# Gates and branch projections with tokens on partitions, their gated sum turned by PE chunk by chunk

## The chip, the cores and the metric

One Trainium2 chip; the kernel runs on one of its cores. PE (TensorE) multiplies matrices, DVE (VectorE) and ACT (ScalarE) work on elements, POOL (GpSimd) does little here, SP (SyncE) issues the loads. Each engine executes its own instructions in order and waits for others by semaphores. The metric is the time of one execution in microseconds (us), the median of three runs.

## The reference, cut to what matters

One layer over x of 256 tokens by 2048 features. h is the normed and modulated x; z = h @ w_in; three branches (mLSTM, differential attention, stick-breaking attention) work on parts of z and give out_m, out_d and out_s of 256 x 1024 each. The change concerns this part:

```python
        merged = (jax.nn.sigmoid(gm) * (out_m @ w_branch[l, 0])
                  + jax.nn.sigmoid(gd) * (out_d @ w_branch[l, 1])
                  + jax.nn.sigmoid(gs) * (out_s @ w_branch[l, 2]))
        x = x + gt1 * (merged @ w_out[l])
```

gm, gd and gs are the last three pieces of z, each 256 x 2048 (columns of w_in). A gated MLP with a depthwise convolution over tokens follows (w_up, w_down), and all of it is float32.

## The kernel before

**Matmuls.** A float32 product is made of three passes: each operand is split in hi, its value rounded to the matmul type fp32r, and lo, the rest; hi*hi, hi*lo and lo*hi are summed in PSUM. Activations are split once; `hh` and `hl` are the hi and lo of h, with features on partitions (16 row tiles of 128 features, 256 tokens each). Weights are streamed: `weights` loads 4 row tiles (4 x 128 rows, 512 columns, tile `raw`, 3 buffers) on SP's queue; ACT casts two row tiles at a time to `hi` (L324) and DVE subtracts to get `lo` (L326); hi and lo have 4 buffers each.

**gemm** makes 512 output columns in two banks of PSUM (pool `gp`, 3 banks) and has two forms. In "F" the output has features on partitions: 128 columns of the weights are the stationary operand and the 256 tokens of the activation stream past (L359). In "T" the output has tokens on partitions: 128 tokens of the activation are stationary and 512 columns of the weights stream past (L357). For one row tile of weights F has 4 column tiles x 3 products, T has 2 token tiles x 3 products. Apart from the last group of a gemm, the two row tiles of a hi/lo pair are done for all output tiles before the next pair.

**Order of the work.** The program emits gemms one after another; between them `tick` emits pieces of two queues: `side` (the generators `stick`, `diff` and `mlstm`, the attention work of the branches) and `ada` (steps that stream w_ada through DVE, L212, for the modulation vectors), at the rates in `rates`. A scheduler then puts every engine's instructions in order.

**Stages around the change**, after the first part of w_in: gates of gs (4 chunks of 512 columns, 16 row tiles each) beside stick and then diff; branch 2 (4 chunks, 8 row tiles each, activation `osh`, `osl`); the sigmoid of mo and the values mv of mLSTM (form T, two chunks each, the end of diff beside them); mq and mk with their convolution (form F); branch 1, each chunk with its gates of gd, beside mlstm; branch 0, each chunk with its gates of gm and, in `ada`, the row gt1; the output projection w_out (form T, 16 row tiles, activation `mgh`, `mgl`). The sum of the gated branches is kept in `mg`, which in `branch` with order 2 is split into mgh and mgl.

**Slots.** Ten large tiles, tags s0 to s9, are used again and again; a new tile in a slot waits until all readers of the old one are done. mg0 and mg1 lie in s8 and s9 (s9 is ez of stick before). od, the output of diff, lies in s2; the transposes `ptf` in `to_features` turn it into odh and odl; `mv` takes s2 next.

Of the kernel before, what the change touches and what calls it, by code (L numbers as in the profile page):

```python
# [12 lines left out]
AF = mybir.ActivationFunctionType  # L13
ALU = mybir.AluOpType
# [3 lines left out]
P = 128  # L18
S = 256
NT = S // P  # L20
D = 2048
KD = D // P
MW = 1024
KM = MW // P
# [11 lines left out]
C_GM, C_GD, C_GS = 10248, 12296, 14344  # L36
# [3 lines left out]
def kernel(  # L40
# [8 lines left out]
    w_ada, w_in, w_out, w_up, w_down = w_ada[0], w_in[0], w_out[0], w_up[0], w_down[0]  # L49
    w_branch = w_branch[0]  # L50
# [16 lines left out]
    def bank(name):  # L67
        return mx.tile([P, 512], F32, tag="mx", name=name)

    def wide(name):  # L70
        return tmp.tile([P, 512], F32, tag="wide", name=name, bufs=3)
# [7 lines left out]
    V, A, T = nc.vector, nc.scalar, nc.tensor  # L79


    ident = const.tile([P, P], F32, name="ident")
# [100 lines left out]
    def pump(queue, n):  # L183
        done = 0
        while queue and done < n:
            try:
                next(queue[0])
                done += 1
            except StopIteration:
                queue.popleft()  # L190

    def drain(queue):
        pump(queue, 1 << 30)
# [3 lines left out]
    def tick():  # L197
        for key, queue in (("ada", ada), ("side", side)):
            state[key] += rates[key]
            n = int(state[key])  # L200
            state[key] -= n
            pump(queue, n)
# [33 lines left out]
    def ada_first(k0):  # L236

        accs = [adap.tile([P, 512], F32, tag="acc", name="acc", bufs=2)]
        for q in range(4):
            raw = rawp.tile([P, 4, 512], F32, tag="raw", name="raw")  # L240
            step = 2 if k0 == 0 and q == 3 else 4
            for j in range(0, 4, step):
                for i in range(2):
                    r0, c0 = q * 512 + j * P, i * D + k0 * P
                    with tc.issue_after(state["load"].ins) if k0 else nullcontext():
                        load = nc.sync.dma_start(raw[:, j:j + step, i * 256:(i + 1) * 256],
                                                 w_ada[r0:r0 + step * P, c0:c0 + 256].rearrange("(k p) f -> p k f", p=P))
            if k0 == 0:
                state["load"] = load
            with tc.issue_after(state["first"].ins) if k0 == 2 and q == 0 else nullcontext():  # L250
                ada_mac(accs, raw, 4 * q, 4)
            yield
        ada_sums(accs, k0, 2)
# [58 lines left out]
    def weights(rows, nk, n, hold=None):  # L312
        if nk == 2:
            raw = adap.tile([P, 2, 512], F32, tag="ada", name="raw2")
        else:
            raw = rawp.tile([P, 4, 512], F32, tag="raw", name="raw")
        with tc.issue_after(state["load"].ins) if not state["started"] else nullcontext():
            state["started"] = True
            state["load"] = nc.sync.dma_start(raw[:, :nk, :n], rows.rearrange("(k p) f -> p k f", p=P))
        his, los = [], []  # L320
        for k0 in range(0, nk, 2):
            hi = hip.tile([P, 2, 512], F32R, tag="hi", name="hi")
            lo = lop.tile([P, 2, 512], F32R, tag="lo", name="lo")
            A.copy(hi[:, :, :n], raw[:, k0:k0 + 2, :n])  # L324
            with tc.issue_after(hold.ins) if hold else nullcontext():
                state["split"] = V.tensor_tensor(lo[:, :, :n], raw[:, k0:k0 + 2, :n], hi[:, :, :n].bitcast(F32),  # L326
                                                 ALU.subtract)
            his.append(hi)
            los.append(lo)
        return his, los  # L330

    def gemm(orient, act, W, row0, col0, n, kt0, kt1, hold=None, hold_all=False, acc=None):

        started = set() if acc is None or kt0 == 0 else {0, 1}
        if acc is None:
            acc = [gp.tile([P, 512], F32, tag="gp", name="gp") for _ in range(2)]
        ah, al = act
        nt = 2 if orient == "T" else n // P  # L340
        per = 1 if orient == "T" else 2

        def mms(t, ks, s0, wh, wl):
            if orient == "T":
                o, sl = acc[t][:, :n], slice(t * P, (t + 1) * P)
            else:
                o, sl = acc[t // 2][:, (t % 2) * S:(t % 2 + 1) * S], slice(t * P, (t + 1) * P)
            for w, acts in ((wh, (ah, al)), (wl, (ah,))):
                for k in ks:
                    wk = w[k // 2][:, k % 2, :]  # L350
                    for a in acts:
                        b = t // per
                        start = b not in started
                        started.add(b)
                        kw = dict(start=start, stop=s0 + k == kt1 - 1 and w is wl, skip_group_check=True)
                        if orient == "T":
                            T.matmul(o, lhsT=a(s0 + k)[:, sl], rhs=wk[:, :n], **kw)  # L357
                        else:
                            T.matmul(o, lhsT=wk[:, sl], rhs=a(s0 + k), **kw)  # L359

        for s0 in range(kt0, kt1, 4):
            nk = min(4, kt1 - s0)
            r0 = row0 + s0 * P
            wh, wl = weights(W[r0:r0 + nk * P, col0:col0 + n], nk, n, hold if s0 > kt0 or hold_all else None)
            last = s0 + nk >= kt1
            for ks in ([range(nk)] if last else [range(k0, k0 + 2) for k0 in range(0, nk, 2)]):
                for t in range(nt):
                    mms(t, ks, s0, wh, wl)
            if not last:
                tick()  # L370
        return acc

    def split(hi, lo, src):

        A.copy(hi, src)
        return V.tensor_tensor(lo, src, hi.bitcast(F32), ALU.subtract)
# [4 lines left out]
    hact = (lambda kt: hh[:, kt, :], lambda kt: hl[:, kt, :])  # L381
# [45 lines left out]
    h0 = ada_first(0)  # L427
# [351 lines left out]

    mg = []  # L780

    def mg_of(ch, b):
        return mg[ch // 2][:, (ch % 2) * 1024 + b * 512:(ch % 2) * 1024 + (b + 1) * 512]

    def gates(col_g, ch, dst):
        acc = gemm("F", hact, w_in, 0, col_g + ch * 512, 512, 0, KD)
        for b in range(2):
            A.activation(dst(ch, b), acc[b], AF.Sigmoid)
        tick()

    def branch(bi, col_g, act, order):
        for ch in range(4):
            if order == 0:
                sg = [mg_of(ch, 0), mg_of(ch, 1)]
            else:
                sg = [wide("sg"), wide("sg")]
                gates(col_g, ch, lambda c_, b: sg[b])
            accb = gemm("F", act, w_branch[bi], 0, ch * 512, 512, 0, KM)
            for b in range(2):
                d = mg_of(ch, b)  # L800
                V.tensor_tensor(sg[b], accb[b], sg[b], ALU.mult)
                if order:
                    V.tensor_tensor(d, d, sg[b], ALU.add)
                if order == 2:
                    h0 = (ch % 2) * 4 + 2 * b
                    split(mgh[ch // 2][:, h0:h0 + 2, :], mgl[ch // 2][:, h0:h0 + 2, :],
                          d.rearrange("p (a t) -> p a t", a=2))
            tick()


# [14 lines left out]
    rates["ada"] = 0.9  # L825
    mg.append(slot(8, "mg0"))
    for ch in range(2):
        gates(C_GS, ch, mg_of)
    drain(side)
    mg.append(slot(9, "mg1"))  # L830
    side.append(diff())
    rates["side"] = 2.6
    for ch in range(2, 4):
        gates(C_GS, ch, mg_of)
    branch(2, C_GS, stick.out, 0)
    drain(side)

# [3 lines left out]
    for ch in range(2):  # L841
        acc = gemm("T", hact, w_in, 0, C_MO + ch * 512, 512, 0, KD)
# [5 lines left out]
    for ch in range(2):  # L848
        acc = gemm("T", hact, w_in, 0, C_MV + ch * 512, 512, 0, KD)
# [5 lines left out]
    for t, col0, f0 in ((mqT, C_MQ, 0), (mkT, C_MK, 8)):  # L855
        for ch in range(2):
            acc = gemm("F", hact, w_in, 0, col0 + ch * 512, 512, 0, KD)
# [9 lines left out]
            for b in range(2):  # L867
                sg = wide("sg")
# [16 lines left out]
    ada.append(ada_row(2, gt1))  # L885
    rates["ada"] = 1.4
    branch(0, C_GM, mlstm.out, 2)


# [8 lines left out]
    for ch in range(4):  # L898
        acc = gemm("T", mact, w_out, 0, ch * 512, 512, 0, KD)
        cs = slice(ch * 512, (ch + 1) * 512)  # L900
        for tt in range(NT):
            t = wide("t512")
# [15 lines left out]
        for k2 in range(2):  # L918
            pb = bank("px2")
            for tt in range(NT):  # L920
                for j in range(2):
                    k = 4 * ch + 2 * k2 + j
                    T.transpose(pb[:, j * S + tt * P:j * S + (tt + 1) * P], x2[tt][:, k * P:(k + 1) * P], ident)  # L923
            for j in range(2):
                k = 4 * ch + 2 * k2 + j
# [7 lines left out]
    for k in range(0, KD, 2):  # L933
# [3 lines left out]
        for j in range(2):  # L937
            b = b2[:, k + j:k + j + 1]
# [9 lines left out]
    for half, (c0, c1) in enumerate(((0, 6), (6, NCH))):  # L948
        ath = [slots.tile([P, 8, S], F32R, tag=f"s{i}", name=f"ath{i}") for i in (0, 3, 4)]
        atl = [slots.tile([P, 8, S], F32R, tag=f"s{i}", name=f"atl{i}") for i in (5, 6, 7)]  # L950
        for ch in range(c0, c1):
# [12 lines left out]
            for b in range(2):  # L964
                sg = wide("sg")
# [11 lines left out]
        act = (lambda kt: ath[kt // 8][:, kt % 8, :], lambda kt: atl[kt // 8][:, kt % 8, :])  # L977
        for n in range(4):
            acc = gemm("T", act, w_down, c0 * 512, n * 512, 512, 0, 4 * (c1 - c0))
            cs = slice(n * 512, (n + 1) * 512)  # L980
            for tt in range(NT):
                t = wide("t512")
# [34 lines left out]
```

## Time and profile before

| | |
|---|---|
| timed runs | 1831.0 us median of 3 (1829.85 to 1831.33) |
| profiled execution | 1832.0 us, span 1830.3 us |
| PE busy | 1792.1 us (98%) |
| DVE busy | 1305.8 us (71%) |
| ACT busy | 878.3 us (48%) |
| DMA | 423.73 MB, mean 232 GB/s |
| chain that ended last | PE 92%, DVE 4%, DMA 3%, issue 1% |
| PE gp L359 (form F) in the chain | 57% |
| PE gp L357 (form T) in the chain | 29% |

Busy is the time in which an engine executes something, as a share of the span. Matmuls overlap, so their single durations add up to more than the time they take, and a busy PE does not say how fast it goes. The chain is followed back from the last instruction, at each step to what it waited for or to the instruction before it on its engine; in a piece of the chain that holds many matmuls of one kind, its length over their number is the pace.

### The profile page before, as it was taken

What the parts mean: (1) busy time and instruction counts of PE and PEld (TensorE: products, weight loads), DVE (VectorE), ACT (ScalarE), POOL (GpSimd) and SP (SyncE); (2) the same over time, 40 slices, a digit from 0 to 9 for tenths busy, and PEclk for the clock granted to TensorE, in tenths of its full rate; (3) what the DMA queues carried; (4) which work ended last, traced back from release to release, by engine and by line L of the source; (5) the groups of instructions that cost most, each with busy time, mean ns of one, the idle gap of its engine ahead of it and who ended that gap; (6) DMA issues with size and microseconds to landing.
All of it is one profiled execution on the core that took longest, in us unless ns stands there. A gap on an engine that the chain in (4) does not pass through costs nothing.

```text
span 1830.3 us, 30158 instructions
## 1 busy us (share of the span) xinstructions
PE 1792.1 (98%) x12453; PEld 1685.4 (92%) x12453; DVE 1305.8 (71%) x1699; ACT 878.3 (48%) x1133; POOL 9.5 (1%) x30
## 2 busy tenths in 40 slices
PE   5989999999999999999999999999999999999998
PEld 4888999999988999999998889999998899999987
DVE  6998867887887677777896566777765555555554
ACT  6533445666564555543444454444443334444432
POOL 0000000000000000000000000000000000000000
PEclk9999999999999999999999999999999999999999
DMA  9988955766687566677996547777755555555563
GB/s 309 337 302 291 316 197 193 245 229 220 223 270 257 184 234 214 226 248 265 315 315 238 186 154 253 251 242 266 263 197 185 197 193 182 182 181 182 192 211 115
DMA packets 219656, 423.73 MB, mean 232 GB/s; under 512 B 8769, under 2 KB 31614, under 8 KB 219006
## 3 DMA queue, kind: packets, MB, share of 16 engines
q1 hardware_dynamic: 217693, 417.56, 67.5%
q8 instruction: 97, 1.59, 0.4%
q0 software_dynamic: 544, 2.11, 0.3%
q10 hardware_dynamic: 1280, 2.14, 0.3%
q14 instruction: 42, 0.34, 0.1%
HBM read 419.68 MB, written 2.10 MB: 230 GB/s over the span
## 4 chain that ended last, share of the span: by engine, by line
PE 92%; DVE 4%; DMA 3%; issue 1%; ACT 0%; SPq 0%; DVEq 0%; ACTq 0%
PE gp L359 57%; PE gp L357 29%; PE kept L359 2%; DMA raw<-in_w_in_dram 1%; DMA raw<-in_w_ada_dram 1%; DVE lo L326 1%; DVE quads L212 1%; DVE acc L212 1%; PE psc L615 0%; ACT hi L324 0%; PE pm L228 0%; PE px L923 0%; PE pr L303 0%; PE pdt L600 0%; PE ptf L673 0%
## 5 line engine op out<-in xcount | busy, mean ns | idle before, releaser
L326 DVE TENSOR_TENSOR lo<-raw,hi 128x1024 fp32r<-128x1024 f32 (+1 forms) x608 | 728.0, 1208 | 387.1 <-ACT hi L324 361.4
L324 ACT CAST hi<-raw 128x1024 fp32r<-128x1024 f32 (+1 forms) x608 | 622.2, 1038 | 737.3 <-PE gp L359 359.9
L359 PE MATMUL gp<-hh,hi 128*128 128x256 f32 x2560 | 664.9, 284 | 3.7 <-ACT skT L487 2.3
L359 PE MATMUL gp<-hl,hi 128*128 128x256 f32 x2560 | 663.5, 284 | 0.0
L359 PEld LDWEIGHTS gp<-hh,hi 128*128 128x128 f32 x2560 | 490.8, 192 | 5.9 <-ACT skT L487 2.5
L359 PEld LDWEIGHTS gp<-hl,hi 128*128 128x128 f32 x2560 | 490.9, 192 | 0.4
L359 PE MATMUL gp<-hh,lo 128*128 128x256 f32 x2560 | 488.2, 284 | 0.5 <-DVE lo L326 0.5
L359 PEld LDWEIGHTS gp<-hh,lo 128*128 128x128 f32 x2560 | 386.7, 192 | 1.1 <-DVE lo L326 0.7
L212 DVE SCALAR_TENSOR_TENSOR acc<-araw,ccol,acc 128x512 f32<-128x512 f32 x240 | 179.0, 746 | 5.2 <-DMA araw<-in_w_ada_dram 3.1
L357 PE MATMUL gp<-hi,hh 128*128 128x440 f32 (+1 forms) x416 | 159.1, 382 | 3.7 <-DVE sv L489 1.1
L357 PE MATMUL gp<-hi,hl 128*128 128x440 f32 (+1 forms) x416 | 157.2, 378 | 0.0
L357 PE MATMUL gp<-hi,atl 128*128 128x512 f32 x352 | 137.0, 389 | 0.0
L357 PE MATMUL gp<-hi,ath 128*128 128x512 f32 x352 | 136.9, 389 | 0.0
L357 PE MATMUL gp<-lo,hh 128*128 128x440 f32 (+1 forms) x416 | 112.6, 377 | 0.9 <-DVE lo L326 0.9
L357 PE MATMUL gp<-lo,ath 128*128 128x512 f32 x352 | 105.8, 389 | 0.0
L357 PEld LDWEIGHTS gp<-hi,hh 128*128 128x128 f32 x416 | 78.7, 189 | 16.2 <-PE gp L357 2.3
L357 PEld LDWEIGHTS gp<-lo,hh 128*128 128x128 f32 x416 | 77.9, 188 | 12.0 <-DVE lo L326 1.9
L357 PEld LDWEIGHTS gp<-hi,hl 128*128 128x128 f32 x416 | 78.8, 189 | 10.3 <-issue 0.7
L357 PEld LDWEIGHTS gp<-hi,ath 128*128 128x128 f32 x352 | 66.1, 188 | 13.8
L357 PEld LDWEIGHTS gp<-lo,ath 128*128 128x128 f32 x352 | 66.1, 188 | 13.7
L357 PEld LDWEIGHTS gp<-hi,atl 128*128 128x128 f32 x352 | 66.1, 188 | 13.7
L212 DVE SCALAR_TENSOR_TENSOR quads<-raw,ccol,quads 128x1024 f32<-128x1024 f32 x45 | 57.5, 1278 | 3.7 <-DMA raw<-in_w_ada_dram 3.6
(338 smaller groups left out, 1738.0 us busy)
## 6 DMA issues: line engine op xcount, KB each, us to landing
raw<-in_w_in_dram SPq DMA_DIRECT2D x98, 1024.0 KB, 5.4
raw<-in_w_up_dram SPq DMA_DIRECT2D x88, 1024.0 KB, 5.2
araw<-in_w_ada_dram SPq DMA_DIRECT2D x128, 512.0 KB, 5.2
raw<-in_w_down_dram SPq DMA_DIRECT2D x44, 1024.0 KB, 5.0
raw<-in_w_ada_dram SPq DMA_DIRECT2D x62, 512.0 KB, 5.0
raw<-in_w_branch_dram SPq DMA_DIRECT2D x24, 1024.0 KB, 5.3
raw<-in_w_in_dram SPq DMA_DIRECT2D x21, 880.0 KB, 4.7
raw<-in_w_out_dram SPq DMA_DIRECT2D x16, 1024.0 KB, 5.0
```

The lines of the kernel that those rows point to most:

```text
L212: V.scalar_tensor_tensor(acc, raw[:, k, :], ccol[:, kt:kt + 1], acc, ALU.mult, ALU.add)
L324: A.copy(hi[:, :, :n], raw[:, k0:k0 + 2, :n])
L326: state["split"] = V.tensor_tensor(lo[:, :, :n], raw[:, k0:k0 + 2, :n], hi[:, :, :n].bitcast(F32), ALU.subtract)
L357: T.matmul(o, lhsT=a(s0 + k)[:, sl], rhs=wk[:, :n], **kw)
L359: T.matmul(o, lhsT=wk[:, sl], rhs=a(s0 + k), **kw)
```

## The change

Gates and branch projections go from form F to form T, so that the sigmoids, the products with the gates and the sum `mg` have tokens on partitions: one chunk of mg is now two tiles of 128 tokens x 512 features. The output projection needs features on partitions, so in branch 0 (order 2) PE transposes each finished chunk of the sum, 128 x 128 at a time, into two banks of PSUM (`pmg`, pool `mx` of 4 banks), and the split into mgh and mgl reads from there. The lines are those of the new kernel from here on where they differ (L811 is the new transpose, L859 the copy to mv that was L851, L679 stays).

```diff
--- before.py
+++ after.py
@@ -779,32 +779,40 @@
 
     mg = []
 
-    def mg_of(ch, b):
-        return mg[ch // 2][:, (ch % 2) * 1024 + b * 512:(ch % 2) * 1024 + (b + 1) * 512]
-
     def gates(col_g, ch, dst):
-        acc = gemm("F", hact, w_in, 0, col_g + ch * 512, 512, 0, KD)
-        for b in range(2):
-            A.activation(dst(ch, b), acc[b], AF.Sigmoid)
+        acc = gemm("T", hact, w_in, 0, col_g + ch * 512, 512, 0, KD)
+        for tt in range(NT):
+            A.activation(dst[tt], acc[tt], AF.Sigmoid)
         tick()
+
+    def mg_of(ch):
+        o = (ch % 2) * 512
+        return [mg[ch // 2][:, tt * 1024 + o:tt * 1024 + o + 512] for tt in range(NT)]
 
     def branch(bi, col_g, act, order):
         for ch in range(4):
             if order == 0:
-                sg = [mg_of(ch, 0), mg_of(ch, 1)]
+                sg = mg_of(ch)
             else:
                 sg = [wide("sg"), wide("sg")]
-                gates(col_g, ch, lambda c_, b: sg[b])
-            accb = gemm("F", act, w_branch[bi], 0, ch * 512, 512, 0, KM)
-            for b in range(2):
-                d = mg_of(ch, b)
-                V.tensor_tensor(sg[b], accb[b], sg[b], ALU.mult)
+                gates(col_g, ch, sg)
+            accb = gemm("T", act, w_branch[bi], 0, ch * 512, 512, 0, KM)
+            for tt in range(NT):
+                d = mg_of(ch)[tt]
+                V.tensor_tensor(sg[tt], accb[tt], sg[tt], ALU.mult)
                 if order:
-                    V.tensor_tensor(d, d, sg[b], ALU.add)
-                if order == 2:
-                    h0 = (ch % 2) * 4 + 2 * b
+                    V.tensor_tensor(d, d, sg[tt], ALU.add)
+            if order == 2:
+                for k2 in range(2):
+                    pb = bank("pmg")
+                    for tt in range(NT):
+                        for j in range(2):
+                            k = 2 * k2 + j
+                            T.transpose(pb[:, j * S + tt * P:j * S + (tt + 1) * P], mg_of(ch)[tt][:, k * P:(k + 1) * P],
+                                        ident)
+                    h0 = (ch % 2) * 4 + 2 * k2
                     split(mgh[ch // 2][:, h0:h0 + 2, :], mgl[ch // 2][:, h0:h0 + 2, :],
-                          d.rearrange("p (a t) -> p a t", a=2))
+                          pb.rearrange("p (a t) -> p a t", a=2))
             tick()
 
 
@@ -825,13 +833,13 @@
     rates["ada"] = 0.9
     mg.append(slot(8, "mg0"))
     for ch in range(2):
-        gates(C_GS, ch, mg_of)
+        gates(C_GS, ch, mg_of(ch))
     drain(side)
     mg.append(slot(9, "mg1"))
     side.append(diff())
     rates["side"] = 2.6
     for ch in range(2, 4):
-        gates(C_GS, ch, mg_of)
+        gates(C_GS, ch, mg_of(ch))
     branch(2, C_GS, stick.out, 0)
     drain(side)
```

What the change does to the order shows at three places.

PE, the first chunk of the gates of gs: its first row tiles before (hi_3116 and lo_3117 are the weights, gp_3112 the first bank, puA and puB belong to stick):

```order
L359 MATMUL gp_3112<-hl_139,hi_3116 128x256
L551 MATMUL puA_2894<-hiA_2886,tri_97 128x512
L553 MATMUL puB_2895<-hlB_2888,tri_97 128x256
L359 MATMUL gp_3112<-hh_138,lo_3117 128x256 x2
L359 MATMUL gp_3112<-hh_138,hi_3116 128x256
```

and now:

```order
L357 MATMUL gp_3112<-hi_3116,hl_139 128x512
L551 MATMUL puA_2894<-hiA_2886,tri_97 128x512
L553 MATMUL puB_2895<-hlB_2888,tri_97 128x256
L357 MATMUL gp_3112<-lo_3117,hh_138 128x512 x2
L357 MATMUL gp_3112<-hi_3120,hh_138 128x512
```

Where a matmul had 256 moving columns of tokens it has 512 moving columns of weights, and after six of them the next row tile pair begins instead of the next column tile.

PE, the end of diff, before: the transposes ptf of od stand in the first chunk of mv (banks gp_5420 and gp_5421), between matmuls of both its token tiles:

```order
L357 MATMUL gp_5421<-hi_5479,hh_138 128x512
L673 MATMUL ptf_5056<-ident_85,od_4098 128x128
L673 MATMUL ptf_5065<-ident_85,od_4098 128x128
L673 MATMUL ptf_5074<-ident_85,od_4098 128x128
L673 MATMUL ptf_5083<-ident_85,od_4098 128x128
L357 MATMUL gp_5421<-hi_5479,hl_139 128x512
L673 MATMUL ptf_5056<-ident_85,od_4098 128x128 x3
L673 MATMUL ptf_5065<-ident_85,od_4098 128x128 x3
```

Now they stand in the second chunk of mv (banks gp_5013 and gp_5014), after 24 matmuls for token tile 0 alone and before the first for token tile 1:

```order
L357 MATMUL gp_5013<-hi_5059,hl_139 128x512
L357 MATMUL gp_5013<-lo_5060,hh_138 128x512 x2
L673 MATMUL ptf_4480<-ident_85,od_3762 128x128
L673 MATMUL ptf_4489<-ident_85,od_3762 128x128
L673 MATMUL ptf_4498<-ident_85,od_3762 128x128
L673 MATMUL ptf_4507<-ident_85,od_3762 128x128
L673 MATMUL ptf_4480<-ident_85,od_3762 128x128 x3
L673 MATMUL ptf_4489<-ident_85,od_3762 128x128 x3
L673 MATMUL ptf_4498<-ident_85,od_3762 128x128 x3
L673 MATMUL ptf_4507<-ident_85,od_3762 128x128 x3
L357 MATMUL gp_5014<-hi_5017,hh_138 128x512
L357 MATMUL gp_5014<-hi_5017,hl_139 128x512
```

The last head of diff (pa, L645 to L647) ends 32 matmuls ahead of the first ptf now; 68 before. On ACT, the same place now, from the copy of the last head to od (pa_4460) to the copies to mv, which come from the banks of the first mv chunk (gp_4844 and gp_4845):

```order
L648 COPY od_3762<-pa_4460 128x2x128
L655 ACTIVATE dsq2_4472<-od_3762 128x2048
L324 CAST hi_5059<-raw_5053 128x1024
L658 ACT_TABLE_LOAD
L658 ACTIVATE ro_4473<-ro_4473,eps_c_110 128x16
L679 ACTIVATE odh_4470<-ptf_4480,cols_131 128x256
L679 ACTIVATE odh_4470<-ptf_4489,cols_131 128x256
L679 ACTIVATE odh_4470<-ptf_4498,cols_131 128x256
L679 ACTIVATE odh_4470<-ptf_4507,cols_131 128x256
L859 COPY mv_4842<-gp_4844 128x2x256
L859 COPY mv_4842<-gp_4845 128x2x256
```

Before, the same steps had 5 weight casts and the two sigmoids of mo between them, and 4 more odh and 3 casts stood ahead of the first copy to mv. On DVE the chain between is the reduction (L656), a lo, an ada step, the reciprocal (L659), an ada step and the two halves of the scaling of od (L663).

PE, the new transposes of the last chunk. Branch 0 ends 6 rows ahead of these (two matmuls of gt1 and four of the output projection lie between); gp_8492 and gp_8493 are the output projection's first chunk:

```order
L357 MATMUL gp_8492<-lo_8497,mgh3_7387 128x512 x2
L357 MATMUL gp_8492<-hi_8500,mgh3_7387 128x512
L357 MATMUL gp_8492<-hi_8500,mgl5_7389 128x512
L357 MATMUL gp_8492<-hi_8500,mgh3_7387 128x512
L357 MATMUL gp_8493<-hi_8496,mgh3_7387 128x512
L357 MATMUL gp_8493<-hi_8496,mgl5_7389 128x512
L357 MATMUL gp_8493<-hi_8496,mgh3_7387 128x512
L811 MATMUL pmg_8460<-ident_85,mg1_3456 128x128 x2
L811 MATMUL pmg_8467<-ident_85,mg1_3456 128x128 x2
```

These four take token tile 0; the four of token tile 1 stand 18 matmuls later. The other three chunks have theirs 15 to 36 matmuls into the next gate chunk.

## Rows read from the trace of the kernel before

**Rows 1.** The page: span, busy time by engine, and GB/s in 40 slices.

```profile
span 1830.3 us, 30158 instructions
...
PE 1792.1 (98%) x12453; PEld 1685.4 (92%) x12453; DVE 1305.8 (71%) x1699; ACT 878.3 (48%) x1133; POOL 9.5 (1%) x30
...
GB/s 309 337 302 291 316 197 193 245 229 220 223 270 257 184 234 214 226 248 265 315 315 238 186 154 253 251 242 266 263 197 185 197 193 182 182 181 182 192 211 115
```

**Rows 2.** The chain, 331 to 420 us: start, length (us), what, number of records.

```profile
by line: PE gp L359 86.2%; PE pdt L600 2.9%; PE po L568 2.9%; PE pzA L527 1.9%; PE po L570 1.5%; PE pzB L529 1.0%; PE puA L552 0.8%; PE puA L551 0.8%; PE pm L218 0.5%; PE puA L555 0.4%; PE puB L553 0.4%; PE puA L556 0.4%; PE puB L554 0.4%
...
344.03 12.35 PE gp L359 x103
356.38 0.23 PE puA L551
```

**Rows 3.** Windows by stage (gates with branch 2; mo, mv; branches 1, 0; two parts).

```profile
core 0: us, PE busy (x) PEld busy (x) DVE busy (x) ACT busy (x) POOL busy (x), PEclk, DMA share, GB/s
331.50:495.40 163.90, 163.90 (x1339) 159.33 (x1339) 134.68 (x211) 103.48 (x162) 0.00 (x0) 1.00 0.68 232
495.40:591.20 95.80, 95.80 (x454) 78.69 (x454) 79.07 (x116) 55.56 (x83) 1.92 (x4) 1.00 0.78 261
...
689.70:979.70 290.00, 290.00 (x2375) 286.72 (x2375) 228.52 (x308) 132.25 (x169) 2.40 (x5) 1.00 0.77 261
370.00:413.00 43.00, 43.00 (x357) 42.78 (x356) 37.24 (x46) 31.01 (x33) 0.00 (x0) 1.00 0.67 227
880.00:945.00 65.00, 65.00 (x541) 64.74 (x541) 56.74 (x69) 28.55 (x34) 0.97 (x2) 1.00 0.92 318
```

**Rows 4.** The chain: long pieces of form T (mv; down) and form F (up).

```profile
557.52 33.60 PE gp L357 x148
...
1355.68 130.60 PE gp L357 x576
1486.28 230.39 PE gp L359 x1920
```

**Rows 5.** Transposes of 128x128: a piece of the chain, and a group by line.

```profile
556.21 1.31 PE ptf L673 x12
```

```profile
L673 PE MATMUL ptf<-ident,num 128*128 128x128 f32 x16 | 2.5, 272 | 0.0
```

**Rows 6.** Groups by line: DVE's half of a split, from SBUF and from PSUM.

```profile
L376 DVE TENSOR_TENSOR mgl<-mg,mgh 128x512 fp32r<-128x512 f32 x8 | 5.5, 686 | 0.7 <-ACT mgh L375 0.7
...
L376 DVE TENSOR_TENSOR osl<-po,osh 128x512 fp32r<-128x512 f32 x4 | 2.8, 692 | 3.2 <-ACT osh L375 3.2
```

**Rows 7.** Timeline of the end of diff, on PE, ACT and DVE: start, length, instruction.

```profile
538.74 0.38 PE L645 MATMUL pa<-dv,aT 128*128 128x128 f32 x2
...
538.72 1.05 ACT L324 CAST hi<-raw 128x1024 fp32r<-128x1024 f32 x1 [1.66 <-PE gp L357]
539.67 0.37 ACT L648 COPY od<-pa 128x256 f32<-128x256 f32 x1
540.07 1.92 ACT L655 ACTIVATE dsq<-od 128x2048 f32<-128x2048 f32 x1
...
556.58 1.57 ACT L679 ACTIVATE odh<-ptf,cols 128x256 fp32r<-128x256 f32 x4 [2.00 <-PE ptf L673]
...
566.67 0.59 ACT L851 COPY mv<-gp 128x512 f32<-128x512 f32 x1 [2.06 <-PE gp L357]
...
542.78 2.28 DVE L656 TENSOR_REDUCE ro<-dsq 128x16 f32<-128x2048 f32 x1
544.97 0.74 DVE L212 SCALAR_TENSOR_TENSOR acc<-araw,ccol,acc 128x512 f32<-128x512 f32 x1
...
548.57 0.24 DVE L659 RECIPROCAL ro<-ro 128x16 f32<-128x16 f32 x1
...
549.35 2.36 DVE L663 TENSOR_TENSOR od<-od,ro 128x1024 f32<-128x1024 f32 x2
551.62 1.22 DVE L326 TENSOR_TENSOR lo<-raw,hi 128x1024 fp32r<-128x1024 f32 x1
```

## Prediction

> **What bounds the kernel now.** I read the page first. PE is busy for 1792.1 of 1830.3 us, 98% of the span [rows 1]. A busy PE need not be PE at its pace, so I went to the chain of work that ended last, in the stretches where gates and branches run. From 331 to 420 us every piece of it is PE work and each piece starts where the one before it ends (344.03 + 12.35 = 356.38) [rows 2]: nothing is waited for there, and a nanosecond taken from PE comes off the end. The windows by stage say the same of all four stages that the change touches or passes: PE 100%, clock 1.00, while DVE has 134.68 of 163.90 us in the first stage (82%) and 228.52 of 290.00 us in branches 1 and 0 (79%) [rows 3]. So the price of a matmul in PE's stream is what counts, and the question behind it is whether the other engines keep up when PE goes faster.
>
> **What the matmuls cost.** The changed chunks are 12 gate chunks of 16 row tiles and 12 branch chunks of 8, 288 row tiles of weights. Form F spends 4 column tiles x 3 products = 12 matmuls of 256 columns on each, T 2 x 3 = 6 of 512. So 3456 F matmuls become 1728 T matmuls, with the same columns in all. The pace of a form comes from long undisturbed pieces of the chain. F: 230.39 us / 1920 = 120.0 ns in the up projection, and 12.35 / 103 = 119.9 ns in the gates themselves. T: 33.60 / 148 = 227.0 ns with the same stationary operand that the gates will have (hh and hl), 130.60 / 576 = 226.7 ns in the down projection [rows 2, 4]. Two F matmuls take 240 ns for the columns that T takes in 227: by these two points a matmul costs 13 ns plus 0.418 ns a column, and the 13 ns is what halving the count saves. The sum: 3456 x 0.120 - 1728 x 0.227 = 414.7 - 392.3 = **22.5 us saved**.
>
> The Trainium skill, "TensorE: Matmul & The Clock Gate", section "Back-to-back issue gap", speaks against this term: it puts the gap of a matmul at its columns over 2.4 GHz plus 2.5 ns. By it F would take 109.2 and T 215.8 ns, and the change would save 1728 x 2.5 = 4.3 us (an estimate from that page). The rows show 120.0 and 227.0 instead, for both forms some 11 ns more [rows 2, 4], so the trace does not agree and I keep its numbers.
>
> **What is added on PE.** 4 chunks x 2 banks x 4 = 32 transposes of 128x128. The same operation stands in the chain at 1.31 us for 12, 109 ns each [rows 5]. 32 x 0.109 = **3.5 us**; if they were not pipelined it would be their mean of 272 ns each, 8.7 us. I take 3.5, because that piece lies inside a gemm as the new ones do. They wait for DVE's sum of each token tile. The order gives the first four of the last chunk 26 matmuls (5.9 us) after its token tile 0 is finished, and the second four 32 (7.3 us) after tile 1 is; DVE's work in between is a product and a sum of some 0.7 us each and a lo or two of 1.22 us, so I cost that wait at nothing. Their results are needed only by row tile 12 of the output projection, 42 matmuls (9.5 us) later.
>
> **What costs nothing.** Sigmoids, products, sums and splits keep their number and shape (128x512). The 8 splits of the sum now read PSUM: 692 ns where such a split reads PSUM against 686 where it reads SBUF [rows 6], 0.05 us in all. Loads are the same, in the same order on SP. If DVE's cover were gone, each of its microseconds would count; see the second rival.
>
> **What the new order costs.** PE executes in order, so I went through the row order for places where PE must wait for the side work that is spread between the gates. In most places the distance between a side step and the next is as long as before in PE time or longer. One is not: the end of diff. Its result od lies in slot 2, which mv takes over. Before, the 16 transposes of od came in the middle of the first mv chunk and nothing waited for mv's slot; the copies to mv came 9 us after. Now diff ends later against PE, after that chunk. Both PSUM banks of the first mv chunk wait for the slot, PE can only run token tile 0 of the next chunk (24 matmuls, until four hi buffers are used up), then the transposes, then nothing until mv is copied. I lay the chain out from the start of the last head's output (time 0), with the durations that the same steps had before [rows 7] and in the order in which ACT and DVE now stand: a weight cast and the copy to od, done at 1.65; the square (1.92) 3.6; the reduction (2.28) 5.9; one lo (1.22) and one ada step (0.74) 7.8; reciprocal, another ada step, and half of the scaling (0.24 + 0.74 + 1.18) 9.9; the other half 11.1. PE has 0.65 us of that head's own and 8 + 24 matmuls of 0.227, 7.9 us: it waits 2.0 us for the first half, does 4 transposes, waits 0.8 us more, does 12 (1.3 us) until 12.4. The four odh pieces (1.57 together, begun as the banks fill) and the copy to mv (0.59) end at 13.9: 1.5 us more. Together **4.3 us** of waiting. The bounds: nothing if DVE and ACT are ahead of this; and if the tail takes as long as it did before, from 538.74 to the last transpose at 557.52 plus 1.57 and 0.59, 20.9 us against 9.6 us of PE work (7.9 and the 16 transposes), 11.3 us. I take 4.3, since in the old order DVE and ACT had no reason to hurry and idled or did other work between those steps.
>
> **Sum.** -22.5 + 3.5 + 4.3 = -14.7 us. The profiled execution took 1832.0 us, its span 1830.3; the median of the three timed runs is 1831.0, 1.0 below. So 1832.0 - 14.7 = 1817.3 for such a profile, and **1816 us** for the median. With the bounds: from -22.5 + 3.5 + 0 = -19.0 (1812) to -22.5 + 8.7 + 11.3 = -2.5 (1828).
>
> **The rivals.**
> 1. DVE becomes the bound in places. From 370 to 413 us it was busy for 37.24 of 43 us, from 880 to 945 for 56.74 of 65 [rows 3]. PE shrinks there by 22.5 / 453.9 = 5%, so these become 91 and 92%, on an engine that executes in order and whose lo's have four buffers of cover. For: the new order puts more of diff's heads beside the sigmoid and mv chunks, where ada runs at a higher rate. Against: T already ran at 227 ns from 495 to 591 us with DVE at 79.07 of 95.80. If the stretches at 90% and more give nothing back, about a third of the 22.5, the time is 1816 + 7.5 = 1823.
> 2. The loads hold branch 0. From 880 to 945 us the DMA engines are busy at 0.92 and move 318 GB/s [rows 3]; with the gain of that stage (22.5 / 3) they would be at 0.97. Against: slices early in the kernel moved 337 GB/s [rows 1]. If they do hold, that third is lost: 1823 again.
> 3. Slower: PE is paid by column, not by instruction. If T in the gates ran at 2 x 120 = 240 ns, nothing would be saved, and 3.5 + 4.3 would stand alone: 1831.0 + 7.8 = 1839. It decides from 240 - 7.8 / 1.728 = 235.5 ns a matmul upwards. Against it stand the two T rows at 227 [rows 4]. If part of the 13 ns is no fixed cost, the gain is that much smaller; a saving of less than 7.8 us gives no gain at all. This is what the page named above would make of it: 1831.0 - 4.3 + 7.8 = 1834.5, an estimate from it. I have no row that shows such a pace.
> That the change doesn't do what it says is excluded by the row order, which shows 512-column matmuls with hh or hl stationary where 256-column ones stood.
>
> **How the numbers follow.** The likeliest case, PE-bound with some waiting, has 0.72 and its own range is 1811 to 1822. Rivals 1 and 2 have 0.12 and 0.06, around 1823 and up to 1827, and nearly all of that is still faster. Rival 3 has 0.05. The last 0.05 is for waits that I did not see in the order, which would bring the time back to where it was. A measurement of this kernel can tell about 0.2% (3.7 us) from no change, so: faster 0.89, same 0.06, slower 0.05. The range 1810 to 1826 leaves out rival 3, the last case and a little of the others.
>
> **What the changed profile would show.** The pieces of the chain in gates and branches at 227 ns a matmul (240 proves rival 3); 32 new transposes at about 109 ns; PE work without gaps but for one place before the second mv chunk's token tile 1, with some 4 us idle around the 16 transposes of od, released by DVE's od and ACT's mv; DVE at about 86% in the first stage and 82% in branches 1 and 0. I am wrong if PE waits for lo or hi in many places (rival 1), for raw in branch 0 (rival 2), or if the wait at od is over 11 us.

## The result, and the profile after

The changed kernel took 1821.83 us (median of 4 runs, 1819.72 to 1822.82); the kernel before, beside it, 1831.16 us (4 runs). The ratio is 0.9942, with a 95% interval of 0.993 to 0.9954: 0.58% faster, 10.6 us of 1831 (8.4 to 12.8). The forecast was 1816 us, in a range of 1810 to 1826. The profiled execution took 1822.27 us, its span 1820.6, 9.7 us below the span in [rows 1].

The page of the changed kernel: span, busy time by engine, shares of the chain.

```profile
span 1820.6 us, 26778 instructions
...
PE 1781.8 (98%) x10757; PEld 1602.3 (88%) x10757; DVE 1304.3 (72%) x1699; ACT 884.1 (49%) x1137; POOL 9.0 (0%) x30
...
PE gp L357 50%; PE gp L359 35%; PE kept L359 2%; DMA raw<-in_w_in_dram 2%; DMA raw<-in_w_ada_dram 1%; DVE lo L326 1%; DVE quads L212 1%; PE psc L615 1%; DVE acc L212 1%; ACT hi L324 0%; PE px L931 0%; PE pm L228 0%; PE ptf L673 0%; PE pr L303 0%; PE pa L640 0%
```

PE has 1696 instructions fewer (1728 matmuls gone, 32 transposes added), and DVE the same number as before. That is the change as it was meant. Its long pieces in the chain, in the gates of gs, in branch 1 and in branch 0 (start, length, what, number):

```profile
404.37 24.08 PE gp L357 x106
...
778.09 49.01 PE gp L357 x216
...
874.97 0.44 PE pmg L811 x4
875.41 24.69 PE gp L357 x108
```

24.08 / 106 = 227.2 ns and 49.01 / 216 = 226.9 ns, the pace of [rows 4]; the transposes of the turn take 0.44 us for four, 109 ns each. In branch 0 it is 228.6 ns (24.69 / 108). The chain of before, in branch 0, held F at 119.3 (34.35 / 288):

```profile
910.13 34.35 PE gp L359 x288
```

So a pair of F matmuls gave back 238.5 - 228.6 = 9.9 ns there, not 13. Both differences lie in the chunks of branch 0 itself, whose activation is omh and oml, the output of mlstm; the gates of gm beside them keep the paces of elsewhere. Before, a chunk of the branch and one of gates, and after, one of gates and one of the branch:

```profile
863.52 11.32 PE gp L359 x96
...
881.06 16.80 PE gp L359 x140
```

```profile
877.95 11.11 PE gp L357 x49
...
889.75 10.35 PE gp L357 x45
```

F takes 117.9 ns with omh and oml and 120.0 in the gates, T 230.0 and 226.7. So already here the pace goes by the tile that is read, and halving the count is worth 5.8 ns a pair with one tile and 13.3 with the other.

Now the windows (columns as in [rows 3]):

```profile
331.00:484.50 153.50, 153.50 (x726) 126.43 (x725) 128.86 (x185) 97.99 (x131) 0.00 (x0) 1.00 0.72 245
880.00:945.00 65.00, 65.00 (x294) 53.44 (x294) 58.21 (x72) 30.10 (x35) 0.97 (x2) 1.00 0.93 314
700.00:970.00 270.00, 270.00 (x1215) 222.17 (x1214) 220.25 (x288) 128.44 (x158) 3.19 (x6) 1.00 0.81 275
```

DVE is busy for 84% of the first window and for 82% of the last, the DMA engines at 0.93 where 0.92 stood before, and PE has no gap in any of them. Neither DVE nor the loads hold PE up.

The gaps are elsewhere. The chain at the end of diff:

```profile
559.39 0.22 PE pa L645 x2
...
560.06 1.41 PE gp L357 x6
...
567.52 2.36 DVE od L663 x2
...
569.93 2.13 PE ptf L673 x12
...
572.45 0.59 ACT mv L859
...
573.08 7.79 PE gp L357 x24
```

and PE's waits from 331 to 592 us (in total, times, longest):

```profile
PE ptf L673 <- DVE od L663: 1.9, 2, 1.5
PE gp L357 <- ACT mv L859: 1.0, 1, 1.0
```

PE waits for the two halves of od (1.9 us) and for the copy to mv (1.0), as the prediction had it. But 24 matmuls behind that wait took 7.79 us, 325 ns each. The windows say why:

```profile
566.00:570.00 4.00, 2.06 (x12) 1.28 (x11) 4.00 (x7) 0.00 (x0) 0.00 (x0) 1.00 0.65 217
570.00:573.00 3.00, 2.04 (x12) 1.64 (x12) 2.88 (x6) 2.23 (x6) 0.12 (x1) 0.62 0.64 236
573.00:575.00 2.00, 1.92 (x5) 1.53 (x6) 1.15 (x4) 1.99 (x6) 0.00 (x0) 0.50 0.00 0
575.00:578.00 3.00, 3.00 (x10) 2.34 (x9) 1.81 (x3) 1.31 (x2) 0.00 (x0) 0.58 0.00 0
578.00:581.00 3.00, 3.00 (x16) 2.38 (x15) 2.18 (x3) 2.32 (x3) 0.00 (x0) 1.00 0.00 0
```

PE idled for half of the first window, and then the granted clock was at 0.50, the 1.2 GHz level, until 578 us.

One more place differs. In each head of diff PE makes score matmuls (psc, L615, 64 rows of the stationary operand) and transposes (pa, L640). Before, and after:

```profile
437.57 0.86 PE psc L615 x8
448.65 0.11 PE pa L640
449.12 0.22 PE pa L640 x2
```

```profile
511.70 0.11 PE pa L640
511.81 0.42 PE psc L615 x2
512.23 0.37 PE pa L640 x2
512.60 0.85 PE psc L615 x4
```

A head took 1.19 us where its scores stood together, and 1.75 us where the transposes of the head before are mixed in. Before, four of the eight heads were mixed with transposes, now seven; over the eight heads these pieces add up to 11.5 us before and 13.8 after.

An account of the profiled execution: -22.5 as forecast, +1.8 for branch 0 (576 pairs at 9.9 ns give 5.7, not 7.5), +3.5 turn, +2.9 waits at od and mv, +2.3 scores, +3.2 lower clock (7.79 - 24 x 0.227 and 2.13 - 1.31) = -8.8. Measured: -9.7. About a microsecond is not followed. The mean granted clock was 0.990 in the profiled execution and 0.993 to 0.995 in the other three, so the stretch at 1.2 GHz is probably not in the median.

### The profile page after: what moved, and what is told of

The parts are those of the page before. It is cut to its first block, busy times and chain, and to the rows that moved or that the text cites. A ratio compares the mean times of both kernels' runs of the same rounds, so it can differ in the third digit from the quotient of the medians.

```text
span 1820.6 us, 26778 instructions
## 1 busy us (share of the span) xinstructions
PE 1781.8 (98%) x10757; PEld 1602.3 (88%) x10757; DVE 1304.3 (72%) x1699; ACT 884.1 (49%) x1137; POOL 9.0 (0%) x30
## 4 chain that ended last, share of the span: by engine, by line
PE 91%; DVE 4%; DMA 3%; issue 1%; ACT 1%; SPq 0%; DVEq 0%; ACTq 0%
PE gp L357 50%; PE gp L359 35%; PE kept L359 2%; DMA raw<-in_w_in_dram 2%; DMA raw<-in_w_ada_dram 1%; DVE lo L326 1%; DVE quads L212 1%; PE psc L615 1%; DVE acc L212 1%; ACT hi L324 0%; PE px L931 0%; PE pm L228 0%; PE ptf L673 0%; PE pr L303 0%; PE pa L640 0%
## 5 line engine op out<-in xcount | busy, mean ns | idle before, releaser
L359 PE MATMUL gp<-hh,hi 128*128 128x256 f32 x1792 | 463.5, 284 | 2.0 <-ACT hh L947 1.3
L359 PE MATMUL gp<-hl,hi 128*128 128x256 f32 x1792 | 464.0, 284 | 0.0
L359 PEld LDWEIGHTS gp<-hh,hi 128*128 128x128 f32 x1792 | 343.6, 192 | 2.8 <-ACT hh L947 1.6
L359 PEld LDWEIGHTS gp<-hl,hi 128*128 128x128 f32 x1792 | 343.8, 192 | 0.2
L359 PE MATMUL gp<-hh,lo 128*128 128x256 f32 x1792 | 339.6, 283 | 0.0
L357 PE MATMUL gp<-hi,hh 128*128 128x512 f32 (+1 forms) x800 | 311.0, 389 | 4.4 <-DVE sv L489 1.4
L357 PE MATMUL gp<-hi,hl 128*128 128x512 f32 (+1 forms) x800 | 308.1, 385 | 0.0
L359 PEld LDWEIGHTS gp<-hh,lo 128*128 128x128 f32 x1792 | 269.9, 192 | 0.3 <-DVE a_c L720 0.3
L357 PE MATMUL gp<-lo,hh 128*128 128x512 f32 (+1 forms) x800 | 229.3, 385 | 0.9 <-DVE lo L326 0.9
L357 PEld LDWEIGHTS gp<-hi,hh 128*128 128x128 f32 x800 | 151.4, 189 | 31.4 <-DVE sv L489 2.2
L357 PEld LDWEIGHTS gp<-hi,ath 128*128 128x128 f32 x352 | 66.1, 188 | 13.7
L357 PEld LDWEIGHTS gp<-hi,atl 128*128 128x128 f32 x352 | 66.1, 188 | 13.7
L357 PEld LDWEIGHTS gp<-lo,ath 128*128 128x128 f32 x352 | 66.1, 188 | 13.7
```

## The experiments

All are compared with the kernel before on the same chip. Since its median moved between 1831.0 and 1832.2 us, the effects below are read from the ratios, times 1831 us.

| run | median, us | ratio (95%) | change, us |
|---|---|---|---|
| changed kernel | 1821.8 | 0.9942 (0.9930 to 0.9954) | -10.6 |
| first_third | 1828.2 | 0.9988 (0.9978 to 0.9997) | -2.2 |
| other_two_thirds | 1823.2 | 0.9956 (0.9943 to 0.9969) | -8.1 |
| turn_twice | 1825.4 | 0.9960 (0.9945 to 0.9974) | -7.3 |
| no_turn | 1817.3 | 0.9919 (0.9904 to 0.9934) | -14.8 |
| scores_together | 1816.7 | 0.9915 (0.9901 to 0.9929) | -15.6 |
| od_slot6 | 1818.1 | 0.9920 (0.9906 to 0.9934) | -14.6 |
| mv_own_slot | 1804.8 | 0.9863 (0.9845 to 0.9880) | -25.1 |
| mv_slot_and_scores | 1799.2 | 0.9822 (0.9805 to 0.9839) | -32.6 |
| before_mv_slot | 1803.2 | 0.9829 (0.9810 to 0.9847) | -31.3 |
| before_pad64 | 1790.3 | 0.9771 (0.9755 to 0.9787) | -41.9 |
| after_pad64 | 1793.1 | 0.9790 (0.9772 to 0.9809) | -38.5 |
| all_three | 1788.6 | 0.9767 (0.9753 to 0.9782) | -42.7 |

### Part of the change: first_third, other_two_thirds

```diff
+    TCOLS = (C_GS,)            # first_third; the other: (C_GD, C_GM,)
     def gates(col_g, ch, dst):
-        acc = gemm("T", hact, w_in, 0, col_g + ch * 512, 512, 0, KD)
+        form = "T" if col_g in TCOLS else "F"
+        acc = gemm(form, hact, w_in, 0, col_g + ch * 512, 512, 0, KD)
...
-            accb = gemm("T", act, w_branch[bi], 0, ch * 512, 512, 0, KM)
+            accb = gemm("T" if col_g in TCOLS else "F", act, w_branch[bi], 0, ch * 512, 512, 0, KM)
```

> Only the gates of gs and branch 2 in form T; branches 1 and 0 with their gates in form F as before, and no turn (the split reads the sum as it lies, so the output mixes two layouts). PE's row order up to the end of mv is that of the changed kernel. Theory: all that the sum missed lies beside diff, which runs in this third: 1152 x 0.120 - 576 x 0.227 = 7.5 us saved, 6.7 us lost at the end of diff (idle, and half the clock behind it) and 2.9 us lost in diff's score matmuls, which stand between the transposes pa now. So 1831.2 - 7.5 + 6.7 + 2.9 = 1833.3 us, slower than before. Rival (the loss is spread over all T pieces, a third of the gain of 9.3 + 2.8 in each stage): 1831.2 - 4.0 = 1827.2 us.

> Gates of gs and branch 2 in form F as before, branches 1 and 0 with their gates in form T and with the turn (the output mixes two layouts). PE's row order around diff is that of the kernel before. Theory: 2304 x 0.120 - 1152 x 0.227 = 15.0 us saved, 2.8 us for the turn, nothing lost: 1831.2 - 15.0 + 2.8 = 1819.0 us. Rival (loss spread over all T pieces): 1831.2 - 8.1 + 2.8 = 1825.9 us.

The first third gave -2.2 us (-4.0 to -0.5), the rest -8.1 (-10.4 to -5.7). I had charged the first third with the lower clock, and this is where the expectation failed: the same waits stand in its trace, but the clock did not fall. PE's waits and the chain behind them in first_third:

```profile
PE ptf L673 <- DVE od L663: 1.9, 2, 1.5
PE gp L357 <- ACT mv L855: 1.2, 1, 1.2
...
573.61 5.74 PE gp L357 x24
```

24 matmuls took 5.74 us, not 7.79. Without the clock the account is -7.5 + 3.1 + 2.3 = -2.1 us, which the run met. For the rest it is -15.0 + 1.8 + 3.5 = -9.7, inside the interval. So less than a third of the first stage's 7.5 us remains, and more than half of the 15.0 of the other two, with the turn paid: the loss lies beside diff, not in all T pieces. Of the six profiles that have this wait, the clock fell in two (of the changed kernel and of after_pad64).

### The turn: turn_twice, no_turn

```diff
                         for j in range(2):
                             k = 2 * k2 + j
-                            T.transpose(pb[:, j * S + tt * P:j * S + (tt + 1) * P], mg_of(ch)[tt][:, k * P:(k + 1) * P],
-                                        ident)
+                            for _ in range(2):
+                                T.transpose(pb[:, j * S + tt * P:j * S + (tt + 1) * P], mg_of(ch)[tt][:, k * P:(k + 1) * P],
+                                            ident)
```

> The changed kernel with each of the 32 transposes of the sum done twice into the same place. By the pace of the traces (88 ns from start to start) 2.8 us more: 1821.8 + 2.8 = 1824.6 us; by the prediction's 109 ns 3.5 us more: 1825.3 us; not pipelined, 272 ns each, 8.7 us more: 1830.5 us.

In no_turn the bank and its transposes are left out, and the split reads `mg_of(ch)[k2]`.

> The changed kernel without the turn: the split reads the sum as it lies, so the output projection works on unturned values. If the turn costs its 32 transposes and no wait, 2.8 us less: 1821.8 - 2.8 = 1819.0 us. Rival: PE also waits for the sums ahead of the turn or for the splits behind it, some 2 us more: 1817 us.

Against the changed kernel, 32 more transposes cost 3.3 us and 32 fewer gave 4.2 us; both intervals are some 3 us wide on either side. The price of 3.5 us by the chain's 109 ns fits both, and so do the 2.8 us by 88 ns; 8.7 us fits neither. Whether a small wait goes with it can't be told from these.

### diff's scores kept together: scores_together

```diff
-                T.transpose(pa[:, b * P:(b + 1) * P], a_[:, b * P:(b + 1) * P], ident)
+                turned = T.transpose(pa[:, b * P:(b + 1) * P], a_[:, b * P:(b + 1) * P], ident)
...
-                    T.matmul(pcs[cc][:, o], lhsT=qT[cp, qs], rhs=kT[cp, ks], start=True, stop=True)
+                    with tc.issue_after(turned.ins) if h else nullcontext():
+                        T.matmul(pcs[cc][:, o], lhsT=qT[cp, qs], rhs=kT[cp, ks], start=True, stop=True)
```

> The changed kernel with diff's score matmuls (psc) of a head issued on PE only after the transposes (pa) of the head before; mv stays in slot 2. Theory: seven heads have their scores mixed with transposes, and the scores and transposes together take 2.9 us more than before; together they run at 0.86 us a head: 1821.8 - 2.9 = 1818.9 us. Rival: scores cost the same wherever they stand: 1821.8 us; or heads come later by the wait for the transposes and diff's end is later still: above 1821.8 us.

5.0 us faster than the changed kernel. The chain of scores_together, the same head as above:

```profile
510.94 0.11 PE pa L641
...
511.29 0.22 PE pa L641 x2
511.51 0.86 PE psc L616 x8
```

1.19 us a head again: eight heads at 1.19 are 9.5 us, 4.3 below the 13.8 of the changed kernel. I had expected only the 2.9 us by which the changed kernel was then counted worse than before; but before had mixed heads too, and those are mended with the others. Each score matmul leaves two records, so the four of a head have eight. Eight in a row take 0.86 us, 107 ns each; the two that stand apart are one matmul's and take 0.42, 210 each. One mixed head of the kernel before has the matmuls of both halves of the 128 rows together between its transposes, and there four records take the same 0.42 us:

```profile
466.70 0.11 PE pa L640
466.81 0.42 PE psc L615 x4
467.24 0.37 PE pa L640 x2
```

So matmuls on different halves run at the same time when they follow each other. The Trainium skill, "TensorE: Matmul & The Clock Gate", section "The mechanism" of Part 3, says that matmuls on different row groups of the array overlap; the trace agrees.

### The wait for od: od_slot6

```diff
-        od = slot(2, "od")[:, 0:2048]
+        od = slot(6, "od")
...
-        oh = slots.tile([P, KM, S], F32R, tag="s6", name="odh")
+        oh = slots.tile([P, KM, S], F32R, tag="s0", name="odh")
...
-        sq2 = slot(0, "dsq2")
+        sq2 = slot(1, "dsq2")
...
-        num = slot(0, "num")
+        num = slot(6, "num")
```

> The changed kernel with od in slot 6 (odh in slot 0, dsq2 in slot 1, num in slot 6): mv in slot 2 has nothing to wait for, all slots keep their sizes and addresses, so the pace of F and T stays 120 and 227 ns. Theory: the 3.0 us of idle PE go, and where the clock fell behind them, its 3 us too: 1821.8 - 3.0 = 1818.8 us, down to 1815.8. Rival (PE then waits elsewhere for the late hi and lo): 1821.8 us.

4.0 us faster than the changed kernel, near the 3.0 expected. In its trace PE runs from the last head through to the transposes and on without a gap:

```profile
560.46 0.22 PE pa L645 x2
...
561.13 16.15 PE gp L357 x71
577.28 0.44 PE ptf L673 x4
...
577.95 1.31 PE ptf L673 x12
579.26 7.30 PE gp L357 x32
```

71 matmuls stand between, at 227 ns, and DVE and ACT, which took 10.5 us for the tail in the changed kernel, are in time. The wait came from the slot that od and mv share.

### Another slot for mv, and a control that fell out otherwise

My first way to remove that wait was to put mv in slot 3:

```diff
-        n = NT * MH * (MDH + 1) + 8 if i == 2 else 2048
-        return slots.tile([P, n], F32, tag=f"s{i}", name=name)
+        n = NT * MH * (MDH + 1) + 8 if i in (2, 3) else 2048
+        t = slots.tile([P, n], F32, tag=f"s{i}", name=name)
+        return t[:, 0:2048] if i == 3 else t
...
-    mv = slots.tile([P, NT, MH, MDH + 1], F32, tag="s2", name="mv")
+    mv = slots.tile([P, NT, MH, MDH + 1], F32, tag="s3", name="mv")
...
-    mqT, mkT = slot(3, "mqT"), slot(4, "mkT")
+    mqT, mkT = slot(2, "mqT")[:, 0:2048], slot(4, "mkT")
```

> The changed kernel with mv in slot 3 (free after branch 2) and mqT in slot 2, so that mv no longer waits for od. PE's row order then has 71 matmuls between the last head and the transposes of od, not 32. Theory: the 3.0 us of idle PE and the time lost at half the clock behind it go together, 6.7 us: 1821.8 - 6.7 = 1815.1 us, and the clock stays at 1.00 there. Rival: DVE and ACT are late themselves, the idle only moves to the next hi or lo, and no more than the 1.0 us that PE waited for mv's copy goes: 1820.8 us.

> As the one with mv in slot 3, and diff's score matmuls (psc) of a head are issued on PE only after the transposes (pa) of the head before, so that the four of them stand together in the order cc 0, cc 1, cc 0, cc 1. Theory: 6.7 and 2.9 us come back: 1821.8 - 9.6 = 1812.2 us. Rival: scores cost the same wherever they stand: the time of the kernel with mv in slot 3 alone (1815.1 by the theory of the slot, 1820.8 by its rival).

> Control: the kernel before with mv in slot 3 and mqT in slot 2. In its trace nothing waits for mv's slot, so no change: 1831.2 us. Rival: the exchange of slots itself moves other waits: off by more than 2 us.

mv_own_slot gained 14.5 us on the changed kernel, more than the wait could hold. The control explains it: the kernel before, where nothing waited for that slot, gained 31.3 us. That no change was expected was wrong, and so was the reason of its rival, as the next pair shows. In this layout the kernel before is not slower than the changed one (-31.3 against -25.1). mv_slot_and_scores gained another 7.5 us, where 2.9 were expected; scores_together had 5.0 for the same edit, and the two do not differ beyond their intervals.

mv needs 64 bytes a partition more than the other slots. So all that is allocated behind slot 3 moved on by 64 bytes, hi and lo among it; hh, hl and slots 2 and 3 stayed. The chain of before_mv_slot in branch 1, first a chunk of the branch alone (stationary hi and lo, moving odh and odl, which moved as well), then gates alone (moving hh and hl, which did not):

```profile
785.72 11.60 PE gp L360 x97
...
797.20 21.91 PE gp L360 x193
```

119.6 ns for the first, 113.5 for the second: the same instruction, 128x256, on the same engine. The pace of F is no property of the instruction alone. Nor is 113.5 all that hh and hl have here: in the up projection of this trace F holds a third pace, 226.13 / 1920 = 117.8 ns.

```profile
1467.66 226.13 PE gp L360 x1920
```

### 64 bytes and nothing else: before_pad64, after_pad64

```diff
+    padp = ctx.enter_context(tc.tile_pool(name="padp", bufs=1))
+    padp.tile([P, 16], F32, name="pad")
     hip = ctx.enter_context(tc.tile_pool(name="hip", bufs=4))
```

> The kernel before with 64 bytes of SBUF left unused ahead of the pool of hi: hi, lo and the small temporary tiles lie 64 bytes further on, no other address and no engine's order changes. Theory (the pace of a matmul depends on how its two operands lie to each other, and the exchange of slots moved them): form F goes from 120.0 to some 113 to 118 ns, T from 227 to 229 to 232. 9216 F matmuls x 2 to 6.5 ns = 18 to 60 us less, 2687 T x 3 ns = 8 us more: between 1780 and 1822 us, near 1803, which the exchange of slots had. Rival (the exchange itself freed a wait, and 13 ns is the fixed cost of an instruction): 1831.9 us and 120.0 ns.

> The changed kernel with the same 64 bytes; every engine's order is that of the changed kernel. Theory: with F at 114.5 and T at 230 ns the change saves 3456 x 0.1145 - 1728 x 0.230 = -1.7 us, so it loses 1.7 us, and 2.8 us for the turn, 2.9 us for the scores and 3.0 us of idle at the end of diff come on top: 10 us slower than the kernel before with the same 64 bytes. Rival (13 ns a matmul in any layout): 9 us faster than it.

before_pad64 gained 41.9 us with no instruction changed and none moved. Its chain: odh's chunk in branch 1, then T in the down projection, and F in the up projection.

```profile
784.33 10.99 PE gp L361 x97
...
1328.55 131.86 PE gp L359 x576
1460.41 217.62 PE gp L361 x1920
```

Now odh's chunk is at 113.3 ns too, where hi has moved and it has not; F in the up projection goes from 120.0 to 113.3, T from 226.7 to 228.9. Two F matmuls take 226.6 ns at this pace, less than one T with 228.9. That the up projection runs at 113.3 here and at 117.8 in before_mv_slot is 8.5 us over those 1920 matmuls, most of the 10.6 by which this run gained more. And after_pad64 is not faster than before_pad64: 0.9790 against 0.9771, +3.5 us, where the intervals of the two overlap. The gain of 9 us of the rival is out of the question. My theory's 10 us more is not reached either. In the two traces the output projection ends, and the up projection starts, at

```profile
1059.04 109.82 PE gp L361 x912
```

before, and at

```profile
1067.83 105.79 PE gp L361 x912
```

after: 8.8 us later, of which the lower clock at the end of diff, which is in this profile, holds about 3. Then the same 912 matmuls take 4.0 us less, in work that neither edit touches. The trace of before_pad64 shows where:

```profile
1069.93 90.10 PE gp L361 x765
...
1169.33 51.70 PE gp L361 x456
```

The first part of its up projection runs at 117.8 ns and the next at 113.4, at full clock, on one line, with hh and hl moving and hi and lo stationary in both; after_pad64 has 113.3 in the first part too (90.21 / 796 behind its start). Some 890 matmuls at 4.4 ns more are 3.9 of the 4.0 us. If that holds for the medians, after_pad64 without them would be some 7 us slower, nearer to the theory. So with 64 bytes F has two paces, and no run shows what chooses between them. Each of the two traces is of its kernel's longest timed run (1794.4 and 1799.1 us); whether the other runs have the same paces at the same places is open.

### All three: all_three

Slot 6 for od, the scores together and the 64 bytes in the changed kernel.

> The changed kernel with three edits of the runs before: od in slot 6, the scores of a head behind the transposes of the head before, and the 64 bytes ahead of hi. If what they gave adds up: 1793.1 - 3.7 - 5.1 = 1784.3 us, below the kernel before with the 64 bytes alone (1790.3). Rival: PE at 114 ns a matmul waits for DVE's lo or the loads in places, and half of it is lost: 1789 us.

1788.6 us, 4.2 us by the ratios below after_pad64, half of the 9.0 that the two edits gave in the old layout, the size that the rival had, though the intervals leave some 4 us on either side. The rival's reason is not in the trace: from 320 to 1050 us PE waits 0.5 us for a lo and 0.3 for a hi. It is the lowest time of the study, but not distinguishable from before_pad64 (0.9767 against 0.9771), which is the old form F with 64 bytes of padding.

## Why the prediction was right, and where it was not

**What bounds.** Right. PE is 98% busy, without gaps in the changed stages, DVE at 84 and 82% where 86 and 82 were forecast, the DMA engines at 0.93. Rivals 1 and 2 did not happen.

**The saving on matmuls, -22.5 us.** T ran at 227 ns in two of the three stages, so the term is nearly right as a number: 20.7 by the chain. It was mis-sized in branch 0, by 1.8 us: I took 120.0 ns from long pieces elsewhere, while the chain of branch 0 itself had 119.3, and T runs there at 228.6, not 227. But the reason given for it fell: "a matmul costs 13 ns plus 0.418 ns a column, and the 13 ns is what halving the count saves". Two points fix a line whatever the cause. With hi and lo 64 bytes further on, F takes 113.3 ns in long stretches and T 228.9, and there halving the count saves nothing. So the condition of the third rival, that part of the 13 ns is no fixed cost, holds, in that layout for all of it and in this one in branch 0; the loss that it made of it did not come. That the term came out all the same is luck: the change left hi, lo, hh and hl where they were. The section "Back-to-back issue gap" of the Trainium skill's page "TensorE: Matmul & The Clock Gate" puts F at 109.2 ns (an estimate from its formula, which it gives for a matmul by itself and not for a stream with weight loads). I had set it aside because the trace showed 120.0; it could have been a hint that these 120.0 held something else. The better layout still stands 4 ns above it for F and 13 ns for T.

**The turn, +3.5 us.** Right: 109 ns each in the chain, +3.3 and -4.2 us by doubling and omission.

**The end of diff, +4.3 us.** Right in place, engines and order; 2.9 us of waiting instead of 4.3, since od was finished 10.5 us after the start of the last head's output (559.39 to 569.88; I had 11.1). The copy to mv ended where it was laid out, 13.7 us after that start (I had 13.9), but PE's 12 transposes, at the lower clock, filled 2.13 us of the time before it instead of 1.3. od_slot6 gives 4.0 us. What I did not count is the clock: PE's idle time there can be followed by a stretch at 1.2 GHz, which cost 3.2 us in the profiled execution and did not occur in first_third.

**"What costs nothing."** Here the prediction failed, by 2.3 us. I compared distances between side steps in PE's order in search of waits. I did not look at which small matmuls stand next to each other, though the order showed it: seven heads of diff instead of four have scores between transposes.

**The sum.** -14.7 was forecast. By the terms as measured it is -20.7 + 3.5 + 2.9 + 2.3 = -12.0, or -8.8 with the lower clock; the ratio says -10.6 (-8.4 to -12.8). The likeliest case of the forecast, PE-bound with some waiting, is what happened, at the upper end of its own range. The waits that came out smaller made up for part of the scores that were left out.

## What to carry to other kernels

A pace read from a trace is a fact about that layout, and about the stretch it was read in, not about the instruction: before halving a count of matmuls to save their "fixed cost", move one operand's pool by 64 bytes and read the pace again. Here that alone gave 41.9 us, four times the change, and took the change's gain away. When an edit shifts a schedule, look for two things in the engine's order: which waits now meet a shared buffer, and which small instructions that overlapped have been separated.

## What the runs showed of the hardware that I had not expected

- The pace of fp32r matmuls depends on where their two operands lie in SBUF, and as far as the runs show on how the two lie to each other. F (128x256): 120.0 ns as built, 113.3 or 117.8 with hi and lo 64 bytes further on, the two paces in one trace with the same operands; T (128x512): 226.7 and 228.9. In before_mv_slot tiles that moved with hi stayed at 119.6 while tiles that stayed behind went to 113.5. Other distances than 64 bytes were not tried, and why it is so stays open.
- Two score matmuls on different halves of the rows run at once when nothing stands between them: eight records in 0.86 us and four in 0.42, against 0.42 us for two of one matmul that are cut off.
- The same idle time of PE (1.9 and 1.0 to 1.2 us) was followed by a granted clock of 0.50 in two of six profiles. A wait of this size may cost as much again.
